# Feed-forward and output projections of a second block: three half-width matmuls per weight tile against one wide and one narrow

## The chip, the cores and the metric

The kernel runs on one core of a Trainium2 chip. The metric is the device time of one execution in microseconds (us); the time before is 1900.26 us, the median of three executions (1900.05 to 1903.23). TensorE is called PE in the profile, its weight loads PEld, VectorE DVE, ScalarE ACT, GpSimd POOL, and SyncE, which starts the transfers, SP.

## What is computed

Two blocks are applied one after the other to 256 tokens of width 1024, in float32. The first block (two layers of retention, neighbourhood attention and grouped attention) is not touched by the change. The second block is what matters here:

```python
def swiglu(x, w_in, w_out):
    g, u = jnp.split(x @ w_in, 2, axis=-1)
    return (jax.nn.silu(g) * u) @ w_out
...
    for i in range(DEPTH):
        h = h + 0.5 * swiglu(rms_norm_2(h, ffn1_norm[i]), ffn1_w_in[i], ffn1_w_out[i])
        hn = rms_norm_2(h, mix_norm[i])
...
            m = recurrent_mixer(hn, ...)
...
            m = spatial_gating_mixer(hn, ...)
        h = h + m
        h = h + 0.5 * swiglu(rms_norm_2(h, ffn2_norm[i]), ffn2_w_in[i], ffn2_w_out[i])
    return rms_norm_2(h, final_norm)
```

`DEPTH` is 2, the hidden width of a feed-forward 2816, that of a mixer 1024. So there are four feed-forwards (each with `w_in` of 1024 x 5632 and `w_out` of 2816 x 1024) and two mixers, each of which ends with a product by an output matrix of 1024 x 1024.

## The kernel before

**Tiling.** Activations lie transposed, 128 features on the partitions and 256 tokens (`T`) in the free dimension: eight tiles for a width of 1024 (`NK`), 22 for the hidden width (`NF`). Every factor of a product is split into two fp32r parts, a rounded hi and the remainder lo (`split`, L387: ACT rounds, DVE subtracts). A product of a weight tile of 128 x 128 and an activation tile takes three matmuls (`mm3`, L400): weight hi by activation hi, weight hi by activation lo, weight lo by activation hi, all added into the same 256 columns of PSUM. Each matmul has its own weight load. `proj` (L439) runs `mm3` over all k tiles of a contraction.

**Stages.** The names in the profile carry the stage: `f` (first feed-forward, input side) and `f0b` (its output side), `mix0r`, `mix0y`, `mix0yb` (recurrent mixer and its output side), `fb` and `fb0b`, `fa` and `fa1b`, `mix` and `mix1b` (spatial mixer), `fb` again and `fb1b`. On the input side (`ffn`, L1251) one step makes one 128-row chunk of the hidden tensor: `project2` (L1207) puts the gate product g and the up product u into the two halves of one PSUM bank of 512 columns, 8 k tiles by three matmuls each, and `ffn_evac` (L1269) multiplies the whole bank by the reciprocal norm `rs`, applies Silu to the g half, multiplies by the u half and splits the result into hi and lo. On the output side (`back`, L1214) each of eight output tiles j has a PSUM bank, half of it used, with 22 k tiles (8 for a mixer); then one DVE instruction adds it to the residual `x[j]`, ACT squares that for the next norm, and `scaled` (L1190) makes the next stage's hi and lo inputs from it: ACT writes hi, DVE lo, side by side in one tile of 512 columns. The weights come in through three `raw` buffers of 1 MB (`wload`), and are split into four `wh` and four `wl` buffers of 1024 columns (`wsplit`, L422). There are eight PSUM banks and 60 tiles in pool `r`.

**Order.** Nothing is issued while the program text runs. A recorder (L96 to L335) keeps every operation, puts them into an order with a list scheduler that knows their dependences, the buffers and a nominal duration for each, and issues each engine's operations in that order; so every instruction has line L335 in the profile, and changed shapes move the order of all engines. At run time each engine takes its own list strictly in order. The scheduler treats operations on one PSUM bank as dependent in program order, so the u half of a bank comes after its g half.

## Time and profile before

| | |
|---|---|
| time, median of 3 executions | 1900.26 us (1900.05 to 1903.23) |
| the profiled execution's own time | 1902.64 us |
| its span, first to last instruction | 1900.9 us |
| PE busy | 1858.4 us, 13632 matmuls |
| DVE busy | 1432.9 us, 2177 instructions |
| ACT busy | 1066.3 us, 1704 instructions |
| mean granted TensorE clock | 0.994 of full speed (2.4 GHz) |
| DMA | 291.95 MB, 154 GB/s |

The profiled execution lies 2.38 us above the median; 1.74 us of its time lie outside its span. Busy time of PE counts overlapping matmuls once; the mean ns of a matmul is its own length from issue to end, longer than the distance from one to the next. How far apart two start is read from the timeline.

### The profile page before, as it was taken

How to read it: one execution, taken by the hardware profiler on the slowest of the kernel's cores; microseconds unless marked ns; L12 is line 12 of the kernel's file. 1: busy time of each engine (PE TensorE's matmuls, PEld its weight loads, DVE VectorE, ACT ScalarE, POOL GpSimd, SP SyncE). 2: the span in 40 equal slices, each digit the busy share in tenths (PEclk: the TensorE clock that was granted, in tenths of full speed). 3: DMA queues.
4: the chain of work that ended last, by engine and by line, in shares of the span. 5: the costliest groups of instructions: out<-in, count | busy, mean ns of one | idle time of the engine just before them, and what ended most of it. 6: DMA issues, size and time to landing. Idle time of an engine off the chain costs nothing.

```text
span 1900.9 us, 33415 instructions
## 1 busy us (share of the span) xinstructions
PE 1858.4 (98%) x13632; PEld 1739.5 (92%) x13632; DVE 1432.9 (75%) x2177; ACT 1066.3 (56%) x1704; POOL 209.7 (11%) x152
## 2 busy tenths in 40 slices
PE   6999999999999999999999999999999999999998
PEld 4888777777789889999999999999999999999998
DVE  7778978799857699999787668876656665777654
ACT  4656555656445597766565447754445444755443
POOL 0123323133300022222000000000000010000000
PEclk9999999999999999999999999999999999999999
DMA  9332443524343324434655566355555555545552
GB/s 321 119 97 93 128 148 101 155 88 123 102 153 100 89 78 116 124 106 146 209 178 188 190 194 200 111 201 187 179 183 180 188 181 193 190 157 176 181 188 98
DMA packets 336249, 291.95 MB, mean 154 GB/s; under 512 B 9184, under 2 KB 325728, under 8 KB 336096
## 3 DMA queue, kind: packets, MB, share of 16 engines
q1 hardware_dynamic: 336096, 289.82, 48.0%
q8 instruction: 107, 1.75, 0.4%
q14 instruction: 46, 0.38, 0.1%
HBM read 288.75 MB, written 1.05 MB: 152 GB/s over the span
## 4 chain that ended last, share of the span: by engine, by line
PE 87%; DVE 8%; ACT 2%; issue 1%; POOL 1%; DMA 0%; SPq 0%; DVEq 0%; POOLq 0%; ACTq 0%
PE fb_ps L335 13%; PE L0m_ps L335 7%; PE f_ps L335 7%; PE fa_ps L335 7%; PE L0n_ps L335 5%; PE L1m_ps L335 5%; PE L1r_ps L335 4%; PE L0r_ps L335 4%; PE fb1b_ps L335 3%; PE L1n_ps L335 3%; PE fa1b_ps L335 3%; PE fb0b_ps L335 3%; PE f0b_ps L335 3%; PE mix_ps L335 3%; PE L0out_ps L335 2%; PE L0in_ps L335 2%
## 5 line engine op out<-in xcount | busy, mean ns | idle before, releaser
L335 PE MATMUL fb_ps<-fb_r,fb_wh 128*128 128x256 f32 x1408 | 253.8, 283 | 0.0
L335 PEld LDWEIGHTS fb_ps<-fb_r,fb_wh 128*128 128x128 f32 x1408 | 219.6, 192 | 0.1
L335 PE MATMUL fb_ps<-fb_r,fb_wl 128*128 128x256 f32 x704 | 198.9, 283 | 0.0
L335 ACT CAST fb_wh<-fb_raw 128x1024 fp32r<-128x1024 f32 x88 | 92.2, 1047 | 123.0 <-PE fb_ps L335 89.3
L335 DVE TENSOR_TENSOR fb_wl<-fb_raw,fb_wh 128x1024 fp32r<-128x1024 f32 x88 | 107.7, 1224 | 65.1 <-ACT fb_wh L335 65.0
L335 PEld LDWEIGHTS fb_ps<-fb_r,fb_wl 128*128 128x128 f32 x704 | 135.0, 192 | 0.0
L335 PE MATMUL f_ps<-f_r,f_wh 128*128 128x256 f32 x704 | 127.2, 283 | 0.0
L335 PE MATMUL fa_ps<-fa_r,fa_wh 128*128 128x256 f32 x704 | 126.9, 283 | 0.0
L335 PE MATMUL L0m_ps<-L0in_r,L0m_wh 128*128 128x512 f32 x384 | 121.5, 395 | 0.0
L335 PEld LDWEIGHTS f_ps<-f_r,f_wh 128*128 128x128 f32 x704 | 109.8, 192 | 0.1
L335 PEld LDWEIGHTS fa_ps<-fa_r,fa_wh 128*128 128x128 f32 x704 | 109.8, 192 | 0.1
L335 PE MATMUL fa_ps<-fa_r,fa_wl 128*128 128x256 f32 x352 | 99.4, 283 | 0.0
L335 PE MATMUL f_ps<-f_r,f_wl 128*128 128x256 f32 x352 | 99.3, 283 | 0.0
L335 PEld LDWEIGHTS L0m_ps<-L0in_r,L0m_wh 128*128 128x128 f32 x384 | 71.9, 189 | 16.7 <-issue 1.6
L335 ACT CAST fa_wh<-fa_raw 128x1024 fp32r<-128x1024 f32 x44 | 46.1, 1047 | 63.5 <-PE fa_ps L335 39.7
L335 DVE TENSOR_TENSOR fa_wl<-fa_raw,fa_wh 128x1024 fp32r<-128x1024 f32 x44 | 53.8, 1224 | 35.4 <-ACT fa_wh L335 35.4
L335 POOL MEMSET mix_r<- 128x128 f32 (+1 forms) x36 | 7.7, 239 | 653.4 <-DVE fa_r L335 490.4
L335 DVE TENSOR_TENSOR L0g_r<-L0g_r,L0g_r 128x512 f32<-128x512 f32 (+3 forms) x116 | 72.4, 670 | 7.6 <-ACT L0g_r L335 5.4
L335 ACT CAST f_wh<-f_raw 128x1024 fp32r<-128x1024 f32 x44 | 46.1, 1048 | 56.4 <-PE f_ps L335 35.6
L335 PE MATMUL L0m_ps<-L0in_r,L0m_wl 128*128 128x512 f32 x192 | 75.0, 391 | 0.0
L335 ACT ACT_TABLE_LOAD x56 | 71.8, 1283 | 3.1 <-PE L0out_ps L335 1.4
L335 DVE TENSOR_TENSOR f_wl<-f_raw,f_wh 128x1024 fp32r<-128x1024 f32 x44 | 53.7, 1221 | 24.9 <-ACT f_wh L335 24.8
(506 smaller groups left out, 5729.7 us busy)
## 6 DMA issues: line engine op xcount, KB each, us to landing
fb_raw<-in_ffn_w_in_dram SPq DMA_DIRECT2D x44, 1024.0 KB, 5.2
f_raw<-in_ffn_w_in_dram SPq DMA_DIRECT2D x22, 1024.0 KB, 5.1
fa_raw<-in_ffn_w_in_dram SPq DMA_DIRECT2D x22, 1024.0 KB, 5.2
ada_raw<-in_ada_w_dram SPq DMA_DIRECT2D x32, 512.0 KB, 4.5
L0m_raw<-in_w_in_dram SPq DMA_DIRECT2D x24, 512.0 KB, 3.9
L1m_raw<-in_w_in_dram SPq DMA_DIRECT2D x24, 512.0 KB, 4.3
L0in_raw<-in_ada_w_dram SPq DMA_DIRECT2D x32, 256.0 KB, 6.0
f0b_raw<-in_ffn_w_out_dram SPq DMA_DIRECT2D x8, 1024.0 KB, 5.3
```

The source lines that it names most:

```text
L335: getattr(getattr(self.real, eng), method)(*a, **k)
```

## The change

On the feed-forwards' input side, and on the output side of feed-forwards and mixers, one matmul of 512 columns takes weight hi by the activation tile [hi|lo] in place of two of 256. All 8 (or 6) k tiles of a weight buffer are taken so, and only then come the matmuls of weight lo by activation hi, 256 columns each, into the first half of the bank. The second half holds weight hi by activation lo, and is added later: on the input side ACT copies it to SBUF and DVE adds the first half (`halves`, twice per chunk, as g and u now have a bank each), and the multiplication by `rs` then reads SBUF; on the output side DVE updates `x[j]` twice, once per half. The hidden tiles are kept as one [hi|lo] tile per 128 rows. The input sides of the mixers and the first block keep three matmuls of 256 columns (`project_pair` is the old `project2`).

```diff
+    def proj_wide(self, out, w, x, k0=0, start=True, stop=True):
+
+        n = len(w)
+        for k in range(n):
+            self.mm(out, lhsT=w[k][0], rhs=x[k0 + k], start=start and k == 0, stop=False)
+        for k in range(n):
+            self.mm(out[:, :T], lhsT=w[k][1], rhs=x[k0 + k][:, :T], start=False, stop=stop and k == n - 1)
+
+    def halves(self, out, ps):
+
+        c = self.f()
+        self.nc.scalar.copy(c[:, :T], ps[:, T:])
+        self.tt(out, ps[:, :T], c[:, :T], ALU.add)
...
+    def project2(self, cols, a):
+
+        out = []
+        for wr in cols:
+            ps = self.ps()
+            self.proj_wide(ps, self.wsplit(wr), a)
+            out.append(ps)
+        return out
+
+    def sums2(self, out, pss, rs):
+
+        for i, ps in enumerate(pss):
+            self.halves(out[:, T * i : T * i + T], ps)
+        self.tt(self.v2(out), self.v2(out), self.b2(rs), ALU.mult)
...
-                self.proj(po[j0 + i][:, :T], self.wsplit(raw[:, :, P * i : P * i + P]), hid, k0,
-                          start=k0 == 0, stop=k0 + kn == kt)
+                self.proj_wide(po[j0 + i], self.wsplit(raw[:, :, P * i : P * i + P]), hid, k0,
+                               start=k0 == 0, stop=k0 + kn == kt)
...
-                self.stt(x[j], po[j][:, :T], scale, x[j], ALU.mult, ALU.add)
+                for h in (slice(0, T), slice(T, T2)):
+                    self.stt(x[j], po[j][:, h], scale, x[j], ALU.mult, ALU.add)
...
-                ps = self.project2(w_in, [g[:, :, c], u[:, :, c]], a)
+                ps = self.project2([g[:, :, c], u[:, :, c]], a)
...
+    def ffn_evac(self, pss, rs, hid):
+        t = self.f()
+        self.sums2(t, pss, rs)
+        s = self.f()
+        self.act(s[:, :T], t[:, :T], AF.Silu)
+        self.tt(s[:, :T], s[:, :T], t[:, T:], ALU.mult)
+        hid.append(self.split_wide(s[:, :T]))
...
-            hid.append(self.pair(s, T))
+            hid.append(self.split_wide(s[:, :T]))
```

How the order moves is shown at three places; a name's last number is its buffer.

PE, in the middle of the third feed-forward's input side (`fa`); before, three matmuls for each activation tile `fa_r`:

```order
L335 MATMUL fa_ps_2896<-fa_r_2832,fa_wh_2897 128x256 x2
L335 MATMUL fa_ps_2896<-fa_r_2832,fa_wl_2898 128x256
L335 MATMUL fa_ps_2896<-fa_r_2833,fa_wh_2897 128x256 x2
L335 MATMUL fa_ps_2896<-fa_r_2833,fa_wl_2898 128x256
L335 MATMUL fa_ps_2896<-fa_r_2834,fa_wh_2897 128x256 x2
L335 MATMUL fa_ps_2896<-fa_r_2834,fa_wl_2898 128x256
```

The same place in the changed kernel, at the end of the eight wide matmuls of one bank:

```order
L335 MATMUL fa_ps_3044<-fa_r_2965,fa_wh_3045 128x512
L335 MATMUL fa_ps_3044<-fa_r_2966,fa_wh_3045 128x512
L335 MATMUL fa_ps_3044<-fa_r_2959,fa_wl_3046 128x256
L335 MATMUL fa_ps_3044<-fa_r_2960,fa_wl_3046 128x256
L335 MATMUL fa_ps_3044<-fa_r_2961,fa_wl_3046 128x256
L335 MATMUL fa_ps_3044<-fa_r_2962,fa_wl_3046 128x256
```

A bank is now one product, g or u; the weight lo is first read eight wide matmuls after the weight hi.

DVE, one chunk of the same stage before (`fa_wl` are weight remainders, the row that reads `fa_ps` is the multiplication by `rs`, the two of 128x256 are the gating product and the hidden tile's remainder):

```order
L335 TENSOR_TENSOR fa_r_2901<-fa_ps_2896,fa_r_2851 128x512
L335 TENSOR_TENSOR fa_wl_2918<-fa_raw_2911,fa_wh_2917 128x1024
L335 TENSOR_TENSOR fa_r_2902<-fa_r_2902,fa_r_2901 128x256
L335 TENSOR_TENSOR fa_wl_2923<-fa_raw_2910,fa_wh_2922 128x1024
L335 TENSOR_TENSOR fa_r_2895<-fa_r_2902,fa_r_2894 128x256
L335 TENSOR_TENSOR fa_r_2908<-fa_ps_2903,fa_r_2851 128x512
```

and one chunk in the changed kernel, where the rows that read `fa_ps` are the two additions and the row of 128x512 after them the multiplication:

```order
L335 TENSOR_TENSOR fa_r_3074<-fa_ps_3068,fa_r_3075 128x256
L335 TENSOR_TENSOR fa_wl_3097<-fa_raw_3091,fa_wh_3096 128x1024
L335 TENSOR_TENSOR fa_r_3065<-fa_r_3064,fa_r_3065 128x256
L335 TENSOR_TENSOR fa_r_3074<-fa_ps_3071,fa_r_3076 128x256
L335 TENSOR_TENSOR fa_r_3074<-fa_r_3074,fa_r_2983 128x512
L335 TENSOR_TENSOR fa_wl_3105<-fa_raw_3090,fa_wh_3104 128x1024
L335 TENSOR_TENSOR fa_r_3077<-fa_r_3077,fa_r_3074 128x256
L335 TENSOR_TENSOR fa_r_3085<-fa_ps_3079,fa_r_3086 128x256
```

The chunk has two rows more, and each addition stands between two weight remainders in the queue.

PE where the spatial mixer's output side starts (`mix1b`); the hidden tiles k = 0, 1, 2 are `mix_r_3228`, `mix_r_3230`, `mix_r_3233` before:

```order
L335 MATMUL mix1b_ps_3247<-mix_r_3228,mix1b_wh_3248 128x256 x2
L335 MATMUL mix1b_ps_3247<-mix_r_3228,mix1b_wl_3249 128x256
L335 MATMUL mix1b_ps_3250<-mix_r_3228,mix1b_wh_3251 128x256 x2
L335 MATMUL mix1b_ps_3247<-mix_r_3230,mix1b_wh_3248 128x256
L335 MATMUL mix1b_ps_3250<-mix_r_3228,mix1b_wl_3252 128x256
L335 MATMUL mix1b_ps_3250<-mix_r_3230,mix1b_wh_3251 128x256
L335 MATMUL mix1b_ps_3256<-mix_r_3228,mix1b_wh_3257 128x256 x2
L335 MATMUL mix1b_ps_3256<-mix_r_3228,mix1b_wl_3258 128x256
L335 MATMUL mix1b_ps_3256<-mix_r_3230,mix1b_wh_3257 128x256
```

In the changed kernel k = 0 to 7 are `mix_r_3426`, `_3428`, `_3431`, `_3433`, `_3436`, `_3438`, `_3441`, `_3443`:

```order
L335 MATMUL mix1b_ps_3445<-mix_r_3426,mix1b_wh_3446 128x512
L335 MATMUL mix1b_ps_3448<-mix_r_3426,mix1b_wh_3449 128x512
L335 MATMUL mix1b_ps_3454<-mix_r_3426,mix1b_wh_3455 128x512
L335 MATMUL mix1b_ps_3457<-mix_r_3426,mix1b_wh_3458 128x512
L335 MATMUL mix1b_ps_3445<-mix_r_3428,mix1b_wh_3446 128x512
L335 MATMUL mix1b_ps_3445<-mix_r_3431,mix1b_wh_3446 128x512
L335 MATMUL mix1b_ps_3445<-mix_r_3433,mix1b_wh_3446 128x512
L335 MATMUL mix1b_ps_3448<-mix_r_3428,mix1b_wh_3449 128x512
L335 MATMUL mix1b_ps_3445<-mix_r_3436,mix1b_wh_3446 128x512
L335 MATMUL mix1b_ps_3445<-mix_r_3438,mix1b_wh_3446 128x512
```

Before, three matmuls of each bank are there for a hidden tile, and one of them needs only its hi part; now one, which reads hi and lo together. DVE at that place in the changed kernel (the first row reads the last PSUM result of the mixer, the rows that write 3428 to 3443 are the remainders):

```order
L335 SCALAR_TENSOR_TENSOR mix_r_3442<-mix_ps_3439,vecs,mix_r_3319 128x256
L335 TENSOR_TENSOR mix_r_3432<-mix_r_3432,mix_r_3409 128x256
L335 TENSOR_TENSOR mix_r_3437<-mix_r_3437,mix_r_3416 128x256
L335 TENSOR_TENSOR mix_r_3440<-mix_r_3440,mix_r_3423 128x256
L335 TENSOR_TENSOR mix_r_3442<-mix_r_3442,mix_r_3423 128x256
L335 TENSOR_TENSOR mix_r_3428<-mix_r_3427,mix_r_3428 128x256
L335 TENSOR_TENSOR mix_r_3433<-mix_r_3432,mix_r_3433 128x256
L335 TENSOR_TENSOR mix_r_3436<-mix_r_3435,mix_r_3436 128x256
L335 TENSOR_TENSOR mix_r_3438<-mix_r_3437,mix_r_3438 128x256
L335 TENSOR_TENSOR mix_r_3441<-mix_r_3440,mix_r_3441 128x256
L335 TENSOR_TENSOR mix_r_3443<-mix_r_3442,mix_r_3443 128x256
```

The remainder of k = 1 is the sixth row, four products behind the row that reads PSUM, and the others follow it.

## Rows read from the trace of the kernel before

**Rows 1.** The page, part 1: an engine's busy us, share of the span, instructions.
```profile
PE 1858.4 (98%) x13632; PEld 1739.5 (92%) x13632; DVE 1432.9 (75%) x2177; ACT 1066.3 (56%) x1704; POOL 209.7 (11%) x152
```

**Rows 2.** Busy time by stage: stretch, its length, busy us (instructions) of PE, PEld, DVE, ACT, POOL, granted clock.
```profile
1164.30:1243.70 79.40, 76.59 (x628) 75.57 (x628) 69.67 (x130) 65.76 (x124) 0.00 (x0) 1.00 0.46 150
...
1434.20:1561.30 127.10, 127.10 (x1060) 127.05 (x1059) 86.66 (x114) 63.51 (x94) 5.59 (x32) 1.00 0.57 187
```

**Rows 3.** The chain that ended last, second block: start us, us, what, matmuls.
```profile
973.38 127.56 PE f_ps L335 x1060
...
1100.93 63.36 PE f0b_ps L335 x528
...
1434.17 127.14 PE fa_ps L335 x1058
...
1561.31 63.36 PE fa1b_ps L335 x528
```

**Rows 4.** Timeline of PE, second block's feed-forward: start us, us, instruction, count.
```profile
1499.94 0.40 PE L335 MATMUL fa_ps<-fa_r,fa_wh 128*128 128x256 f32 x2
...
1507.14 0.40 PE L335 MATMUL fa_ps<-fa_r,fa_wh 128*128 128x256 f32 x2
```

**Rows 5.** Timeline of PE, first block's merge, 512 columns per matmul.
```profile
519.74 0.61 PE L335 MATMUL L0m_ps<-L0in_r,L0m_wh 128*128 128x512 f32 x2
...
526.54 0.62 PE L335 MATMUL L0m_ps<-L0in_r,L0m_wh 128*128 128x512 f32 x2
```

**Rows 6.** Timeline of PE, first block, both widths in turn.
```profile
626.01 0.40 PE L335 MATMUL L1r_ps<-L0out_r,L1r_wh 128*128 128x512 f32 x1
626.25 0.40 PE L335 MATMUL L1r_ps<-L1r_wh,L0out_r 128*128 128x256 f32 x2
626.49 0.28 PE L335 MATMUL L1r_ps<-L1r_wl,L0out_r 128*128 128x256 f32 x1
626.61 0.40 PE L335 MATMUL L1r_ps<-L0out_r,L1r_wh 128*128 128x512 f32 x1
```

**Rows 7.** Groups by form, third feed-forward: busy us, mean ns, idle before and releasers.
```profile
L335 DVE TENSOR_TENSOR fa_wl<-fa_raw,fa_wh 128x1024 fp32r<-128x1024 f32 x42 | 51.4, 1224 | 31.7 <-ACT fa_wh L335 31.7
...
L335 ACT CAST fa_wh<-fa_raw 128x1024 fp32r<-128x1024 f32 x41 | 42.9, 1047 | 57.5 <-PE fa_ps L335 39.7 <-issue 13.5 <-DMA fa_raw<-in_ffn_w_in_dram 4.2
...
L335 DVE TENSOR_TENSOR fa_r<-fa_ps,fa_r 128x512 f32<-128x512 f32 x21 | 14.4, 690 | 5.3 <-PE fa_ps L335 5.3
...
L335 DVE TENSOR_TENSOR fa_r<-fa_r,fa_r 128x256 f32<-128x256 f32 x21 | 8.7, 418 | 0.0
...
L335 ACT CAST fa_r<-fa_r 128x256 fp32r<-128x256 f32 x21 | 8.3, 401 | 0.0
```

**Rows 8.** PE's waits in the second block: us in total, times, longest.
```profile
PE mix0yb_ps L335 <- DVE mix0y_r L335: 1.0, 1, 1.0
PE mix0yb_ps L335 <- DVE mix0yb_r L335: 0.9, 1, 0.9
PE mix0yb_ps L335 <- DVE mix0yb_wl L335: 0.5, 1, 0.5
PE mix0yb_ps L335 <- ACT mix0yb_wh L335: 0.4, 1, 0.4
PE fb1b_ps L335 <- DVE fb1b_r L335: 0.3, 1, 0.3
```

**Rows 9.** Timeline of PE (first row) and DVE where mix1b starts.
```profile
1677.21 0.40 PE L335 MATMUL mix1b_ps<-mix_r,mix1b_wh 128*128 128x256 f32 x2
...
1677.47 0.48 DVE L335 SCALAR_TENSOR_TENSOR mix_r<-mix_ps,vecs,mix_r 128x256 f32<-128x256 f32 x1
...
1677.87 3.43 DVE L335 TENSOR_TENSOR mix_r<-mix_r,mix_r 128x256 f32<-128x256 f32 x10
...
1682.35 0.42 DVE L335 SCALAR_TENSOR_TENSOR L0out_m<-mix1b_ps,L0out_m 128x256 f32<-128x256 f32 x1
```

More of the change, by code (lines that the diff above doesn't have):

```diff
@@ L1197, in scaled, with split_wide @@
             self.stt(lo, x[j], wj, hi.bitcast(F32), ALU.mult, ALU.subtract)
-            out.append((hi, lo))
+            out.append(t)
         return out
+    def split_wide(self, src):
+        t = self.r()
+        self.split(t[:, :T], t[:, T:], src)
+        return t
     def b2(self, r):
@@ L1205, in v2, with project_pair @@
         return t.rearrange("p (a b) -> p a b", a=2)
-    def project2(self, w, cols, a):
+    def project_pair(self, cols, a):
         ps = self.ps()
+        x = [(t[:, :T], t[:, T:]) for t in a]
         for i, wr in enumerate(cols):
-            self.proj(ps[:, T * i : T * i + T], self.wsplit(wr), a)
+            self.proj(ps[:, T * i : T * i + T], self.wsplit(wr), x)
         return ps
+    def project2(self, cols, a):
[9 more added lines that the diff above has]
+        self.tt(self.v2(out), self.v2(out), self.b2(rs), ALU.mult)
     def back(self, w_out, hid, x, scale, halves=0, then=None):
@@ L1255, in ffn @@
             (u,) = self.wload([self.wk(w_in, D_FF + P * f, 256)])
-            th, tl = self.r(), self.r()
             for i in range(2):
                 c = slice(P * i, P * i + P)
-                ps = self.project2(w_in, [g[:, :, c], u[:, :, c]], a)
+                ps = self.project2([g[:, :, c], u[:, :, c]], a)
                 if f == 0 and i == 1:
                     rs = mk_rs()
-                    self.ffn_evac(first, rs, th, tl, 0, hid)
+                    self.ffn_evac(first, rs, hid)
                 elif f == 0:
@@ L1265, in ffn @@
                     continue
-                self.ffn_evac(ps, rs, th, tl, i, hid)
+                self.ffn_evac(ps, rs, hid)
         return self.back(w_out, hid, x, 0.5, then=then)
-    def ffn_evac(self, ps, rs, th, tl, i, hid):
-                t = self.f()
-                self.tt(self.v2(t), self.v2(ps), self.b2(rs), ALU.mult)
-                s = self.f()
-                self.act(s[:, :T], t[:, :T], AF.Silu)
-                self.tt(s[:, :T], s[:, :T], t[:, T:], ALU.mult)
-                c = slice(T * i, T * i + T)
-                self.split(th[:, c], tl[:, c], s[:, :T])
-                hid.append((th[:, c], tl[:, c]))
+    def ffn_evac(self, pss, rs, hid):
[5 more added lines that the diff above has]
+        hid.append(self.split_wide(s[:, :T]))
     def softplus(self):
@@ L1330, in chain @@
             (raw,) = self.wload([self.wk(w, D + P * jp, 256)])
-            ps = self.project2(w, [raw[:, :, P * i : P * i + P] for i in range(2)], a)
+            ps = self.project_pair([raw[:, :, P * i : P * i + P] for i in range(2)], a)
             if jp == 0:
@@ L1375, in gated @@
             (raw,) = self.wload([self.wk(w, P * jp, 256)])
-            ps = self.project2(w, [raw[:, :, P * i : P * i + P] for i in range(2)], a)
+            ps = self.project_pair([raw[:, :, P * i : P * i + P] for i in range(2)], a)
             y = self.f()
@@ L1381, in gated @@
             self.tt(y, y, hs[jp // 2], ALU.mult)
-            hi, lo = self.pair(y, 512)
             for i in range(2):
-                hid[jp + i] = (hi[:, T * i : T * i + T], lo[:, T * i : T * i + T])
+                hid[jp + i] = self.split_wide(y[:, T * i : T * i + T])
         self.early = EARLY
@@ L1419, in spatial @@
                     tk = slice(P * t, P * t + P)
-                    self.mm3(ps[:, T * t : T * t + T], (a[k][0][:, tk], a[k][1][:, tk]), ws[k], k == 0, k == NK - 1)
+                    self.mm3(ps[:, T * t : T * t + T], (a[k][:, :T][:, tk], a[k][:, T:][:, tk]), ws[k], k == 0, k == NK - 1)
             if cc == 0:
@@ L1433, in spatial @@
             (raw,) = self.wload([self.wk(w, P * jp, 256)])
-            ps = self.project2(w, [raw[:, :, P * i : P * i + P] for i in range(2)], a)
+            ps = self.project_pair([raw[:, :, P * i : P * i + P] for i in range(2)], a)
             u = self.f()
```

## Prediction

> **What bounds the kernel now.** The page's first part comes first: PE is busy for 98% of the span, DVE for 75% [rows 1]. Busy is not yet the bound, so the chain that ended last is read next, from the start of the second block at 973 us. It shows one engine with nothing between: 127.56 us of PE for the first feed-forward's input side, 63.36 us for its output side, and the same in the later ones, stage after stage [rows 3]. 63.36 us for 528 matmuls are 120.0 ns each; 127.14 us for 1056 and the norm's two matmuls are the same pace. The table by stage agrees: in the third feed-forward PE is busy 127.10 of 127.10 us at granted clock 1.00 (2.4 GHz), while DVE works 86.66 us and ACT 63.51 us [rows 2]. The list of PE's waits in the whole second block has five entries between 0.3 and 1.0 us, 3.1 us together, four of them in the recurrent mixer's output side and one at the end [rows 8]. So in the 915 us where the change acts, the time is the number of matmuls times their distance, as long as DVE and ACT keep ahead.
>
> Then the distance itself, from the timeline. In the second block the listed rows from 1499.94 to 1507.14 us hold 20 rows of two matmuls and 20 of one, 60 of 256 columns in 7.20 us: 120.0 ns each [rows 4]. In the first block's merge, matmuls of 512 columns with the same kind of weight load run from 519.74 to 526.54, 30 in 6.80 us: 226.7 ns each [rows 5]. Twice the columns cost 106.7 ns more, not 120.0. So a matmul pays 106.7 ns per 256 columns and 13.3 ns besides, whatever its width. Where both widths take turns nothing is added: a wide one starts at 626.01, two narrow ones at 626.25, one at 626.49, the next wide one at 626.61 [rows 6], that is 0.24, 0.24 and 0.12 us.
>
> **What the change gives.** A pair of weight tile and activation tile costs 3 x 120.0 = 360.0 ns now, and 226.7 + 120.0 = 346.7 ns after: 13.3 ns less, with the same columns streamed and one weight load fewer. The pairs: a feed-forward has 44 products of 8 k tiles on the input side and 8 of 22 on the output side, 528; four have 2112; two mixers' output sides add 2 x 64. **2240 pairs x 13.3 ns = 29.9 us.** All of it lies on PE, which is the chain there. Bounds for the price of a wide matmul in these stages: 226.7 ns [rows 5] and twice 120.0 [rows 4], at which the gain is nothing. I take 226.7, since rows 5 have the same shape and types, fp32r weights, 512 contiguous columns and one whole bank, and rows 6 mix the widths.
>
> The Trainium skill, "TensorE: Matmul & The Clock Gate", section "Wait — 56ns, not 53.3ns?", puts the fixed cost of a warm matmul at about 2.5 ns beyond its columns. By it the change would save 2240 x 2.5 = 5.6 us; the measured distances of both widths [rows 4, 5] disagree with it, and the measurement decides.
>
> **What it adds beside PE.** A chunk of the input side gets two ACT copies of 256 from PSUM and two DVE additions of 256. No row shows just these: a 256-wide DVE product is 0.42 us in SBUF, a 512-wide one out of PSUM 0.69 [rows 7], a 256-wide update out of PSUM 0.42 [rows 9]; a 256-wide ACT rounding is 0.40 [rows 7]. I take 0.42 and 0.40; the upper ends are 0.69 for DVE and, for ACT, half of its 1.05 us for 1024 columns. A stage has 44 of each: DVE 86.7 + 44 x 0.42 = 105.2 us, ACT 63.5 + 17.6 = 81.1, both within the 122.0 us that PE then needs (352 x 346.7 ns). With 0.69 DVE has 117, still below. The multiplication by rs keeps its 512 columns. Two banks per chunk instead of one still leave four chunks in the eight banks, and a bank is now emptied before rs is needed, so the first chunks don't wait for the norm. Cost on the path: nothing, and the cover is PE's 5.55 us per chunk. The weights' low parts are needed 8 x 0.227 = 1.8 us later than their high parts, which helps. Transfers keep their order and sizes; they come 2% faster at a DMA share of 0.57 [rows 2].
>
> **What goes onto the path.** Three places.
>
> First, the spatial mixer's output side. Now PE starts it at 1677.21, the last result leaves PSUM on DVE from 1677.47, and then come ten rows of 0.34 us, products and remainders, until 1681.3 [rows 9]; PE doesn't wait, because it takes many matmuls that need only the hi part of a hidden tile. A wide matmul needs both. The changed order gives PE four wide matmuls (0.9 us, to 1678.1), then k = 1, whose remainder is the fifth of the ten rows: 1677.87 + 5 x 0.34 = 1679.6. **1.5 us lost**; afterwards remainders come every 0.34 us and PE asks for one in 0.23 to 0.45, so nothing more. Bounds: 0, if DVE is earlier, and 3.2, if PE waits until 1681.3.
>
> Second, the recurrent mixer's output side, where PE already idles 2.8 us of 79.4 [rows 2, 8] on DVE's tiles and on weight splits. What PE saves there (64 x 13.3 ns = 0.85 us) is mostly waited for again: **0.65 us lost**, between 0 and 0.85.
>
> Third, the end. After the last matmul DVE has two updates for each of the last two output tiles instead of one: 2 x 0.42 [rows 9], both in front of the last transposes: **0.8 us lost**, 0.4 if one is hidden.
>
> At the other stage starts the last two inputs come up to 0.8 us later, by the extra updates, with a weight remainder of 1.2 us queued between. After its last matmul DVE needs three updates, that remainder and the input's own: 3 x 0.42 + 1.22 + 0.48 = 3.0 us. The new orders put 19 or 20 wide matmuls, 4.3 us, ahead of the first that reads them. Cost: nothing; 1.9 us per start if the cover is gone.
>
> **The sum.** 29.9 - 1.5 - 0.65 - 0.8 = 26.9 us. Against the profiled execution 1902.64 - 26.9 = 1875.7 us; that execution stands 2.4 us above the median, so for the median 1900.26 - 26.9 = **1873.4 us**, 1.4% faster.
>
> **Rivals.**
>
> *Late starts.* At five stage starts (four feed-forwards, the spatial mixer) PE waits for the last two inputs. For it: DVE's queue is in order, and two updates and a weight remainder stand in front of them. Against: the cover of 4.3 us. Price: 5 x 1.9 = 9.5 us, so 1882.9.
>
> *DVE takes over, and the kernel gets slower.* In a stage DVE's 86.7 us of work already come with 37 us in which it stood, 31.7 for ACT's roundings and 5.3 for PE [rows 7], 124 of 127. An addition is late when its copy is late, and the weight remainder queued behind it is late with it. If the waits stay as they are, a stage takes 86.7 + 37.0 + 18.5 = 142.2 us instead of 127.1; four stages lose 60 us, output sides and mixers still give 11.1 back, the three places take 2.95: about 1952. It decides from 21.9 us of waits per stage on (127.1 - 105.2), and above 16.8 it eats into the gain. Against it: ACT's roundings stand 39.7 us for PE to free weight buffers [rows 7], so DVE's waits are mostly those of engines that run ahead, and shrink when there is more to do.
>
> *Only a small fixed cost goes.* If the 13.3 ns belong to something that the wide form keeps here, and 2.5 ns per pair go, 5.6 us less 2.95 us leave 1897.6. Against: rows 4 and 5.
>
> *It doesn't do what it says.* The wide form streams at the pace of two narrow ones: 1900.26 + 2.95 = 1903.2. Against: rows 5.
>
> **How the numbers follow.** About 0.2%, 3.8 us, is what a measurement of this kernel can tell from no change. My forecast (1868 to 1879) gets 0.74, late starts and partial delays of the evacuation (1879 to 1893) 0.15, the small fixed cost 0.03, no effect 0.03, the slower case 0.05. Faster by over 0.2% (below 1896.5) is the first two and part of the third, 0.90; within 0.2% 0.05; slower 0.05. The range starts where nothing is lost and the recurrent mixer's 2.8 us of idle time go too, 1900.26 - 29.9 - 2.8 = 1867.6; it ends past the late starts (1882.9) with the bounds of the first place (1.7 more): 1885. What is left out is 0.11 for the last three rivals and a few hundredths of partial delays.
>
> **What the profile after would show.** PE with 13632 - 2240 = 11392 matmuls. In the timeline of a feed-forward, wide rows 0.227 us apart and then narrow ones 0.120 apart; chain pieces of about 122.4 us for an input side and 61.0 for an output side, still PE alone. DVE near 105 us and ACT near 81 in a stage. PE's waits: one of about 1.5 us at the start of mix1b, those of mix0yb a little longer, none of note in a feed-forward. It is wrong if wide matmuls stand 0.24 us apart, if the chain of a feed-forward holds DVE or ACT pieces, or if waits for fa_r or fa_wl appear in every chunk.

## The result, and the profile after

| | before | after |
|---|---|---|
| median, us | 1901.72 | 1882.11 |
| lowest to highest, us | 1900.05 to 1903.23 | 1880.28 to 1883.12 |
| profiled execution, us | 1902.64 | 1883.12 |
| its span, us | 1900.9 | 1881.1 |

Both columns are four executions, taken side by side. The ratio is 0.9896 with an interval of 0.9879 to 0.9913: about 1.0% faster, 19.6 us between the medians. The sum of the prediction had 26.9 us, so some 7 us of the expected gain have to be found.

The first part of the page of the changed kernel shows the matmuls that went (13632 before, [rows 1]) and the work that came to DVE and ACT:

```profile
PE 1837.5 (98%) x11392; PEld 1623.5 (86%) x11392; DVE 1504.0 (80%) x2405; ACT 1114.0 (59%) x1884; POOL 209.9 (11%) x152
```

The chain that ended last, from the start of the second block on (start us, us, engine and tile, matmuls), answers to [rows 3]:

```profile
975.44 123.76 PE f_ps L335 x708
1099.20 61.52 PE f0b_ps L335 x352
...
1239.23 123.28 PE fb_ps L335 x706
1362.52 61.50 PE fb0b_ps L335 x352
1424.01 123.37 PE fa_ps L335 x706
1547.38 61.48 PE fa1b_ps L335 x352
1608.86 52.23 PE mix_ps L335 x434
1661.12 2.90 DVE mix_r L335 x8
1664.06 21.72 PE mix1b_ps L335 x124
1685.78 123.32 PE fb_ps L335 x706
1809.10 62.98 PE fb1b_ps L335 x364
```

The feed-forwards are PE alone, as forecast. But their pieces are 123.3 to 123.8 us where 122.4 were expected, and 61.5 where 61.0 were. The block starts at 975.44 instead of 973.38, though nothing ahead of it was changed.

Two stretches by stage, with the columns of [rows 2] (length, busy us of PE, PEld, DVE, ACT, POOL, granted clock): the recurrent mixer and the third feed-forward's input side.

```profile
1160.70:1239.20 78.50, 76.71 (x564) 73.27 (x563) 71.07 (x140) 66.89 (x128) 0.00 (x0) 0.98 0.46 148
1424.00:1547.40 123.40, 123.40 (x708) 108.56 (x707) 101.37 (x159) 74.97 (x136) 5.21 (x32) 1.00 0.59 193
```

DVE has 101.4 us of work in 123.4 and ACT 75.0; PE is never without work. In the mixer the granted clock is 0.98 where it was 1.00, and PE is as long busy with 564 matmuls as it was with 628.

PE's waits in the second block, beside [rows 8]:

```profile
PE mix0yb_ps L335 <- DVE mix0y_r L335: 1.7, 1, 1.7
PE mix1b_ps L335 <- DVE mix_r L335: 1.6, 1, 1.6
PE fb1b_ps L335 <- DVE fb1b_r L335: 1.1, 2, 0.8
```

PE's timeline inside the third feed-forward, beside [rows 4] (start us, us, instruction, count):

```profile
1480.18 2.00 PE L335 MATMUL fa_ps<-fa_r,fa_wh 128*128 128x512 f32 x8
1482.02 1.11 PE L335 MATMUL fa_ps<-fa_r,fa_wl 128*128 128x256 f32 x8
1482.97 2.00 PE L335 MATMUL fa_ps<-fa_r,fa_wh 128*128 128x512 f32 x8
1484.81 1.12 PE L335 MATMUL fa_ps<-fa_r,fa_wl 128*128 128x256 f32 x8
1485.77 2.00 PE L335 MATMUL fa_ps<-fa_r,fa_wh 128*128 128x512 f32 x8
```

From one bank's first wide matmul to the next one's are 2.79 us, 349 ns a pair. Eight times 226.7 and eight times 120.0 would be 2.774. The starts of the single matmuls in the same trace, averaged over the full banks of this stage, show where the 20 ns are: the distances behind the eight wide ones are 233.3, 235.5, 228.4, 232.6, 230.8, 226.8, 226.8 and 226.7 ns, those behind the narrow ones 113.5, 119.2 and then 120.0. (For the first one 233.3 is the value of the output sides; in this stage one bank with a wait of 0.2 us lifts its mean.) The first five wide matmuls are slow, by 27 ns together, and the first narrow one gives 6.5 back. On an output side, where no bank is emptied in the meantime, the distances are the same within 0.3 ns; in its parts of six wide and six narrow ones the loss is 20 ns too.

**Where the 26.9 us went.** In the second block, from its start in the chain to the end of the span, 927.5 us became 905.7: 21.8 us gained. The other 2.1 us are the later start. So in the block 5.1 us are missing: 288 runs of wide matmuls (176 banks of the input sides, 96 parts of the feed-forwards' output sides, 16 of the mixers') with 20 ns each make 5.7 us, and the three places where something was to be added cost about what the sum had, somewhat less in the first mixer.

The later start came in code that both kernels have. Against the trace of before, the same matmuls of the first block slip by 0.8 us near 27 us of the span and by 0.95 us between 420 and 422, and hardly elsewhere. The second place is visible by stage: first before, then after.

```profile
420.00:440.00 20.00, 18.79 (x109) 13.28 (x110) 17.95 (x26) 9.63 (x15) 1.90 (x1) 0.91 0.67 198
```

```profile
420.00:440.00 20.00, 17.59 (x101) 11.84 (x101) 17.01 (x24) 8.96 (x14) 0.00 (x0) 0.83 0.63 185
```

In that execution the granted clock stood longer at half there, and near 27 us it rose later. In all the profiled executions of this study the second block's piece of the chain began between 971.4 and 975.5 us, with the same first block. That is the spread of the runs, not the change. For this reason the table below gives the second block by itself.

### The profile page after: what moved, and what is told of

Same layout as the page of the kernel before. It is cut to its first block, busy times and chain, and to the rows that moved or that the text cites. A ratio compares the mean times of both kernels' runs of the same rounds, so it can differ in the third digit from the quotient of the medians.

```text
span 1881.1 us, 29398 instructions
## 1 busy us (share of the span) xinstructions
PE 1837.5 (98%) x11392; PEld 1623.5 (86%) x11392; DVE 1504.0 (80%) x2405; ACT 1114.0 (59%) x1884; POOL 209.9 (11%) x152
## 4 chain that ended last, share of the span: by engine, by line
PE 88%; DVE 7%; ACT 2%; issue 1%; DMA 1%; POOL 1%; SPq 0%; DVEq 0%; POOLq 0%; ACTq 0%
PE fb_ps L335 13%; PE L0m_ps L335 8%; PE f_ps L335 7%; PE fa_ps L335 7%; PE L0n_ps L335 5%; PE L1m_ps L335 5%; PE L1r_ps L335 4%; PE L0r_ps L335 4%; PE fb1b_ps L335 3%; PE L1n_ps L335 3%; PE f0b_ps L335 3%; PE fb0b_ps L335 3%; PE fa1b_ps L335 3%; PE mix_ps L335 3%; PE L0out_ps L335 2%; PE L0g_ps L335 2%
## 5 line engine op out<-in xcount | busy, mean ns | idle before, releaser
L335 PE MATMUL fb_ps<-fb_r,fb_wh 128*128 128x512 f32 x704 | 176.6, 393 | 0.0
L335 PEld LDWEIGHTS fb_ps<-fb_r,fb_wh 128*128 128x128 f32 x704 | 126.7, 189 | 22.8
L335 PE MATMUL fb_ps<-fb_r,fb_wl 128*128 128x256 f32 x704 | 98.1, 282 | 0.0
L335 PE MATMUL f_ps<-f_r,f_wh 128*128 128x512 f32 x352 | 88.7, 393 | 0.0
L335 PE MATMUL fa_ps<-fa_r,fa_wh 128*128 128x512 f32 x352 | 88.4, 393 | 0.0
L335 ACT CAST fa_wh<-fa_raw 128x1024 fp32r<-128x1024 f32 x44 | 46.1, 1050 | 47.6 <-PE fa_ps L335 29.9
L335 PEld LDWEIGHTS fa_ps<-fa_r,fa_wh 128*128 128x128 f32 x352 | 63.4, 189 | 11.4
L335 DVE TENSOR_TENSOR fa_wl<-fa_raw,fa_wh 128x1024 fp32r<-128x1024 f32 x44 | 53.8, 1223 | 24.4 <-ACT fa_wh L335 18.1
L335 PEld LDWEIGHTS f_ps<-f_r,f_wh 128*128 128x128 f32 x352 | 63.4, 189 | 11.4
L335 PE MATMUL L1m_ps<-L0out_r,L1m_wh 128*128 128x256 f32 x384 | 71.8, 283 | 0.0
L335 ACT CAST L0m_wh<-L0m_raw 128x1024 fp32r<-128x1024 f32 (+1 forms) x48 | 39.9, 837 | 53.1 <-PE L0m_ps L335 35.0
L335 DVE TENSOR_TENSOR L0n_r<-L0n_r,L0n_r 128x512 f32<-128x512 f32 (+2 forms) x104 | 69.8, 714 | 1.1 <-POOL L0n_r L335 0.5
```

The source lines that it names most:

```text
L335: getattr(getattr(self.real, eng), method)(*a, **k)
```

## The experiments

Theory: TensorE's distances set the time, the wide form saves 13.3 ns a pair, and a fixed 20 ns is lost at each change from a run of narrow matmuls to wide ones. Rivals: the loss belongs to the start of a bank, to each wide matmul, or to the evacuation that reads the banks meanwhile; or the gain is not one of the width at all.

All runs in one table. "Second block" goes from its first matmul to the last instruction of the profiled execution; "fa" and "fa1b" are the input and the output side of the third feed-forward, from first matmul to first matmul.

| kernel | median us | ratio to before (95%) | second block us | fa | fa1b |
|---|---|---|---|---|---|
| before | 1901.72 | | 927.60 | 127.14 | 63.36 |
| after | 1882.11 | 0.9896 (0.9879 to 0.9913) | 905.77 | 123.37 | 61.48 |
| alternate | 1876.77 | 0.9859 (0.9845 to 0.9874) | 900.89 | 122.68 | 61.04 |
| two_banks | 1880.64 | 0.9882 (0.9867 to 0.9896) | 906.29 | 122.92 | 61.26 |
| no_halves | 1879.69 | 0.9880 (0.9865 to 0.9894) | 905.67 | 123.36 | 61.48 |
| input_only | 1884.16 | 0.9902 (0.9885 to 0.9918) | 910.08 | 123.39 | 63.36 |
| three_narrow | 1902.27 | 1.0001 (0.9992 to 1.0011) | 927.28 | 127.26 | 63.36 |
| fours | 1884.17 | 0.9910 (0.9895 to 0.9925) | 908.51 | 123.87 | 61.65 |
| twos | 1879.40 | 0.9886 (0.9869 to 0.9902) | 905.94 | 123.06 | 61.35 |
| alternate_mix0 | 1876.77 | 0.9870 (0.9851 to 0.9890) | 906.39 | 122.47 | 61.05 |
| all_wide | 1882.13 | 0.9889 (0.9874 to 0.9905) | 911.34 | 122.68 | 61.05 |
| after_again | 1880.77 | 0.9886 (0.9871 to 0.9900) | 905.78 | 123.37 | 61.48 |
| alternate_again | 1877.29 | 0.9868 (0.9852 to 0.9884) | 903.96 | 122.68 | 61.05 |
| mixers_narrow | 1879.22 | 0.9880 (0.9865 to 0.9895) | 904.18 | 123.37 | 61.48 |

### Is the gain one of the width? three_narrow

```diff
 (proj_wide)
-        for k in range(n):
-            self.mm(out, lhsT=w[k][0], rhs=x[k0 + k], start=start and k == 0, stop=False)
-        for k in range(n):
-            self.mm(out[:, :T], lhsT=w[k][1], rhs=x[k0 + k][:, :T], start=False, stop=stop and k == n - 1)
+        for a, b in ((0, 0), (0, 1), (1, 0)):
+            for k in range(n):
+                self.mm(out[:, :T], lhsT=w[k][a], rhs=x[k0 + k][:, T * b : T * b + T],
+                        start=start and a + b + k == 0, stop=stop and a == 1 and k == n - 1)
 (sums2)
-            self.halves(out[:, T * i : T * i + T], ps)
-        self.tt(self.v2(out), self.v2(out), self.b2(rs), ALU.mult)
+            self.tt(out[:, T * i : T * i + T], ps[:, :T], rs[:, :T], ALU.mult)
 (back)
-                for h in (slice(0, T), slice(T, T2)):
+                for h in (slice(0, T),):
```

> The order of the changed kernel (all k of one product, then the next) with matmuls of 256 columns throughout: eight hi x hi, eight hi x lo, eight lo x hi, all into the first half of the bank, so that nothing has to be added later. If the gain is the fixed 13.3 ns of the matmuls that went: 360.0 ns a pair and 2.880 us a bank as before the change, input sides of the feed-forwards 127.1 us, output sides 63.4; in all within 0.2% of the kernel before (1900 to 1905). Rival, the gain (or a part) comes of the order or of weights that change less often: below 1895, at the limit 1882.

1902.27 us, 1.0001 of before. The stages are those of before: 127.26 and 63.36 us. The changed order, with its own banks for gate and up, is worth nothing by itself. The whole gain hangs on the 512 columns.

### Where do the 20 ns belong? alternate and two_banks

In alternate, each k's narrow matmul stands behind its wide one:

```diff
         for k in range(n):
             self.mm(out, lhsT=w[k][0], rhs=x[k0 + k], start=start and k == 0, stop=False)
-        for k in range(n):
             self.mm(out[:, :T], lhsT=w[k][1], rhs=x[k0 + k][:, :T], start=False, stop=stop and k == n - 1)
```

> The wide and the narrow matmul of each k stand one behind the other instead of eight wide, then eight narrow. In the changed kernel a bank of eight pairs takes 2.793 us where its single durations (8 x 226.7 + 8 x 120.0 ns) make 2.774: 20 ns more in each of 280 banks, 5.5 us. Theory A, a fixed loss at every change from narrow to wide: eight changes a bank instead of one, 7 x 20 ns x 280 = +38 us on 1882.1, about 1920, a pair at some 366 ns. Theory A', the loss settles over the five wide matmuls that follow a change and the first of them bears only 6.6 ns, which the narrow one behind it gives back: a pair at 346.7 ns, 1876.6. Rivals B (a loss at the start of each accumulating bank) and C (every wide matmul is 2.5 ns dearer than in the first block's rows): still 349 ns a pair, about 1882.

1876.77 us, 0.9859: theory A' named 1876.6, the fixed loss per change (1920) is out, and so are B and C (1882). That the number is hit so closely is in part luck: this order has a second, slower pace, which came up in later runs (see the versions further on). PE's timeline of alternate in the third feed-forward:

```profile
1479.71 0.39 PE L335 MATMUL fa_ps<-fa_r,fa_wh 128*128 128x512 f32 x1
1479.94 0.28 PE L335 MATMUL fa_ps<-fa_r,fa_wl 128*128 128x256 f32 x1
1480.06 0.39 PE L335 MATMUL fa_ps<-fa_r,fa_wh 128*128 128x512 f32 x1
1480.29 0.28 PE L335 MATMUL fa_ps<-fa_r,fa_wl 128*128 128x256 f32 x1
...
1483.18 0.39 PE L335 MATMUL fa_ps<-fa_r,fa_wh 128*128 128x512 f32 x1
```

From 1479.71 to 1483.18 are ten pairs: 347 ns each, the 346.7 of the prediction. 900.89 us for the second block are 26.7 less than before.

In two_banks the wide matmuls of two banks come first, then the narrow ones of both:

```diff
+        n = len(ws[0])
+        for out, w in zip(outs, ws):
+            for k in range(n):
+                self.mm(out, lhsT=w[k][0], rhs=x[k0 + k], start=start and k == 0, stop=False)
+        for out, w in zip(outs, ws):
+            for k in range(n):
+                self.mm(out[:, :T], lhsT=w[k][1], rhs=x[k0 + k][:, :T], start=False, stop=stop and k == n - 1)
```

> The wide matmuls of two banks (gate and up, or two output tiles) come first, then the narrow ones of both: half as many changes from narrow to wide, as many bank starts. Theory A (loss at a change of width, 20 ns): 140 changes fewer, -2.7 us, about 1879.4; the wide matmuls of the second bank 226.7 ns apart from the first on, two banks in 5.567 us. Rival B (loss at the start of a bank): the second bank's first five wide matmuls are as slow as the first's (233, 236, 228, 233, 231 ns), two banks in 5.587 us, 1882.1. Rival C (each wide matmul): the loss is spread over all sixteen, 1882.1.

Its timeline in the third feed-forward:

```profile
1483.48 3.82 PE L335 MATMUL fa_ps<-fa_r,fa_wh 128*128 128x512 f32 x16
1487.13 2.08 PE L335 MATMUL fa_ps<-fa_r,fa_wl 128*128 128x256 f32 x16
1489.05 3.14 PE L335 MATMUL fa_ps<-fa_r,fa_wh 128*128 128x512 f32 x13
```

Two banks take 5.57 us, theory A's figure. In the single starts the second bank's eight wide matmuls, which begin a bank of their own, are 226.7 ns apart from the first on; only those behind the narrow run are slow. So the loss is not at the start of a bank and not in each wide matmul. The stages gain by it (122.92 against 123.37 us), but the whole came to 1880.64 instead of 1879.4, with an interval that holds both: in the profiled execution PE also waited 1.8 us for f_r and 0.9 for mix_r at two stage starts where the changed kernel doesn't.

### Is it the evacuation? no_halves

```diff
         for i, ps in enumerate(pss):
-            self.halves(out[:, T * i : T * i + T], ps)
-        self.tt(self.v2(out), self.v2(out), self.b2(rs), ALU.mult)
+            self.tt(out[:, T * i : T * i + T], ps[:, :T], rs[:, :T], ALU.mult)
```

> On the input sides of the four feed-forwards the second half of each bank (weight hi x inputs' lo) is left out of the sum: no ACT copy and no DVE add, and the rs multiply reads the bank's first half. The matmuls stay. If the matmuls alone set the pace there: the same time within 0.2% (1880 to 1884), 2.793 us a bank, DVE some 18 us less busy in each input stage. Rival D, the evacuation's reads of the banks are what slows the first five wide matmuls: 2.774 us a bank, 3.4 us faster over 176 banks, about 1878.7. Rival E, DVE's added work delays PE: faster by more than that.

The same stretch by stage, in no_halves:

```profile
1423.20:1546.50 123.30, 123.30 (x708) 108.45 (x707) 87.90 (x139) 65.81 (x95) 5.56 (x32) 1.00 0.59 192
```

DVE has 13.5 us less to do and ACT 9.2, and the stage takes the same time: 123.36 us against 123.37. The median, 1879.69, is just below the expected bracket; the second block, 905.67 against 905.77 us, is the same, and the rest is the first block's spread. The adding of the halves costs nothing on the path. DVE still reads the first half of each bank here, so this run alone doesn't exclude the reads; but the loss is the same on the output sides, where no bank is emptied in the meantime, and so the reads of the banks are not what slows the wide matmuls.

### How long a run does it take? twos and fours

```diff
+        for k1 in range(0, n, 4):
+            ks = range(k1, min(k1 + 4, n))
-        for k in range(n):
+            for k in ks:
                 self.mm(out, lhsT=w[k][0], rhs=x[k0 + k], start=start and k == 0, stop=False)
-        for k in range(n):
+            for k in ks:
                 self.mm(out[:, :T], lhsT=w[k][1], rhs=x[k0 + k][:, :T], start=False, stop=stop and k == n - 1)
```

(in twos a 2 stands for the 4)

> Four wide, four narrow, four wide, four narrow. Alternating single matmuls took 346.7 ns a pair and lost nothing; runs of six, eight and sixteen narrow ones lose 20 ns at the change to wide. If a run of four already brings the whole loss: two changes a bank, up to 20 ns each, a bank 2.807 to 2.813 us, 1886 to 1888. If the loss grows with the run and is half for four: 2.793, 1882. If it needs more than four in a row: 2.774, 1876.6.

> Two wide, two narrow, four times a bank. If any run of narrow ones longer than one brings the loss, cut off after the two wide that follow (6.6 + 9.0 - 6.5 ns a change): 2.810 us a bank, 1887. If the loss grows with the run, a quarter of 20 ns for two: 2.793, 1882. If runs this short lose nothing: 2.774, 1876.6.

Timeline of fours:

```profile
1479.79 1.09 PE L335 MATMUL fa_ps<-fa_r,fa_wh 128*128 128x512 f32 x4
1480.72 0.63 PE L335 MATMUL fa_ps<-fa_r,fa_wl 128*128 128x256 f32 x4
1481.19 1.09 PE L335 MATMUL fa_ps<-fa_r,fa_wh 128*128 128x512 f32 x4
1482.12 0.64 PE L335 MATMUL fa_ps<-fa_r,fa_wl 128*128 128x256 f32 x4
1482.60 1.09 PE L335 MATMUL fa_ps<-fa_r,fa_wh 128*128 128x512 f32 x4
```

and of twos:

```profile
1479.75 0.63 PE L335 MATMUL fa_ps<-fa_r,fa_wh 128*128 128x512 f32 x2
1480.22 0.40 PE L335 MATMUL fa_ps<-fa_r,fa_wl 128*128 128x256 f32 x2
1480.45 0.63 PE L335 MATMUL fa_ps<-fa_r,fa_wh 128*128 128x512 f32 x2
...
1481.84 0.63 PE L335 MATMUL fa_ps<-fa_r,fa_wh 128*128 128x512 f32 x2
```

Fours take 2.81 us a bank, the first of their three cases in pace; the time, 1884.17 us, stayed below its 1886 to 1888. Twos take 0.697 us for two pairs, 2.787 a bank, a little under their middle case, and 1879.40 us. From the single starts the loss at one change is 3.3 ns in runs of two, 14 to 16 in runs of four, and 20 in runs of six, eight and sixteen; per pair that is 1.7, 3.5 to 4, 3.3, 2.5 and 1.3 ns.

These runs shorten the wide stretch together with the narrow one, and the first block of the kernel before, which has no such link, separates the two. There four narrow matmuls between long wide stretches (from 491.96 us) are followed by distances of 233, 236, 229, 232 and 231 ns: four already bring the whole loss. In fours only four wide ones follow, and the first four slow distances less what the narrow ones give back make 15.7 ns. So from four on theory A', cut off where the wide stretch ends, is right; for two it would give some 9 ns where 3.3 were measured, and that stays open.

### The parts: input_only and mixers_narrow

```diff
 (back, input_only)
-                self.proj_wide(po[j0 + i], self.wsplit(raw[:, :, P * i : P * i + P]), hid, k0,
+                self.proj(po[j0 + i][:, :T], self.wsplit(raw[:, :, P * i : P * i + P]), [(t[:, :T], t[:, T:]) for t in hid], k0,
...
-                for h in (slice(0, T), slice(T, T2)):
-                    self.stt(x[j], po[j][:, h], scale, x[j], ALU.mult, ALU.add)
+                self.stt(x[j], po[j][:, :T], scale, x[j], ALU.mult, ALU.add)
```

In mixers_narrow the same stands under `if kt == NK`, which is true in the mixers alone.

> The output sides go back to three narrow matmuls a pair and one update a tile; only the input sides are wide. 832 pairs lose 360.0 - 349.2 = 10.8 ns each, +9.0 us; what came back are the waits at the starts of the output sides, 1.6 us in mix1b, some 0.7 of mix0yb's 1.7, 0.8 of fb1b: -3.1. About +5.9 on 1882.1, 1888.0. If the late starts are not worth that much (the work behind them was waiting anyway): 1891. If the output sides' gain was already lost elsewhere: 1883 or less.

> The changed kernel with the output sides of both mixers back at three narrow matmuls a pair and one update a tile; the feed-forwards stay wide. 128 pairs x 10.8 ns = 1.4 us lost. If the late starts are the price of the wide form there, mix1b goes from 24.2 to 23.25 us and the first mixer from 78.5 to 76.7, as in the run with only the input sides wide: 2.8 us faster than the changed kernel, about 1879.3. If not, 1883.5.

input_only came to 1884.16 us, not 1888. Its output sides are back at 63.36 us, as expected, and mix1b at 23.25 (24.22 in the changed kernel). The recurrent mixer is the miss: 76.72 us, 1.8 shorter than in the changed kernel, where the expectation had let its waits and its pairs cancel. The second block is 4.3 us longer than the changed kernel's, against 5.9 expected, and in the profiled execution it began 2.7 us earlier.

mixers_narrow: 1879.22 us beside 1880.77 of the changed kernel on the same chip, 1.6 us faster (second block 904.18 against 905.78) where 2.8 were expected. The first mixer went to 77.80 us instead of 76.7, mix1b to 23.25. PE's waits there:

```profile
PE mix0yb_ps L335 <- ACT mix0y_r L335: 0.7, 1, 0.7
PE mix0yb_ps L335 <- DVE mix0yb_r L335: 0.4, 1, 0.4
PE mix0yb_ps L335 <- DVE mix0y_r L335: 0.2, 1, 0.2
```

So with all wide matmuls of a bank in a row, the two mixers' output sides together lose more by their starts than their 128 pairs give, 1.6 us of the second block; the executions of the two kernels overlap (1878.97 to 1880.61 and 1879.66 to 1881.13 us).

But it is not the width that makes mix1b late. three_narrow also runs one bank through all its k before the rest, with matmuls of 256 columns alone, and its mix1b takes 24.19 us, as in the changed kernel:

```profile
PE mix1b_ps L335 <- ACT mix_r L335: 0.9, 1, 0.9
```

And alternate, which is wide but takes the narrow matmul of each k before the next k, has mix1b at 23.18 us, a little under the narrow 23.25, with a wait of 0.6 us. So the late start comes with the order, which needs the later hidden tiles early. In the first mixer the price of the wide form can't be told apart: with narrow matmuls on its output side it took 79.4 us (before), 77.9 (alternate_mix0), 77.8 (mixers_narrow), 77.2 (three_narrow) and 76.7 (input_only), with wide ones 78.2 to 79.3, and the order of DVE and ACT is another in each.

### Versions further on: alternate_mix0, all_wide, and three kernels on one chip

alternate_mix0 has the order of alternate and the narrow form in the recurrent mixer's output side. all_wide has in addition:

```diff
-            ps = self.project_pair([raw[:, :, P * i : P * i + P] for i in range(2)], a)
+            ps = self.project2([raw[:, :, P * i : P * i + P] for i in range(2)], a)
...
-            self.tt(self.v2(rt), self.v2(ps), self.b2(S["rs"]), ALU.mult)
+            self.sums2(rt, ps, S["rs"])
```

> Wide and narrow alternate as in the run of that name (1876.77 us, 0.9859 of before), and the output side of the first mixer goes back to three narrow matmuls a pair and one update a tile. With the output sides narrow the first mixer took 76.7 us, with the alternating order 78.4: 1.7 us faster than alternating alone, about 1875, 0.985 of before. If the waits at the start of mix0yb come from elsewhere: 64 pairs x 13.3 ns = 0.85 us slower than alternating, 1877.6.

> As alternate_mix0, and the input sides of both mixers are wide too, alternating, with the ACT copy and the DVE add for their 24 banks. 24 x 8 = 192 pairs x 13.3 ns = 2.6 us where TensorE sets the pace: about 1872.5, 0.9835 of before. If DVE and ACT, which the first mixer's chain of small steps loads most, take the added work onto the path: 24 x (0.37 + 0.42) us is 19 us of added work, of which the first mixer has two thirds, and the time is anywhere from 1875 to 1885, slower than alternate_mix0.

all_wide: 1882.13 us, the second case. PE's longest waits in its first mixer:

```profile
PE mix0y_ps L335 <- DVE mix0y_r L335: 2.5, 1, 2.5
...
PE mix0yb_ps L335 <- DVE mix0yb_r L335: 1.6, 1, 1.6
```

From its first matmul to the next stage's it takes 84.8 us, against 77.9 in alternate_mix0, which differs by the mixers' input sides alone. There too the chain goes over ACT and DVE for much of the stage. So where DVE and ACT bound a stage, the added work (16 copies of 0.37 us and 16 additions of 0.42) made it 6.9 us longer, and the matmuls saved did not make up for it.

alternate_mix0: 1876.77 us, no faster than alternating alone, with executions from 1873.20 to 1883.54. In the profiled one (1883.54) the recurrent mixer is 0.5 us shorter, where 1.7 were expected, but f takes 125.68 us, f0b 62.03, fb 124.84 and fb0b 62.08, where the run of alternate has 123.67, 61.07, 122.54 and 61.08. The matmuls and their order in these stages are the same. The single starts show why: from one wide matmul to the next are 353.3 ns in the first four feed-forward stages (the expectation below says three), and 346.7 in the later ones. The next three kernels were run for that.

> The alternating order once more. A profiled run of it took 346.7 ns a pair in all stages, one of alternate_mix0 353.8 ns in the first three feed-forward stages and 346.7 behind them. If each stage falls into one of two paces when TensorE starts it, the runs lie between 1873 (all at 346.7) and 1884 (most at 353.8; 2112 pairs x 7.1 ns = 15 us between the ends), with a median of 1875 to 1880, under the changed kernel's, and wider than its. If the slower pace belongs to alternate_mix0 alone: 1873 to 1878.5 again.

> The changed kernel as it is, beside the next two on one chip: 1880 to 1884 us, 0.9885 to 0.991 of before; 349.2 ns a pair in every feed-forward stage, as the loss comes at the same place of each bank.

alternate_again: 1877.29 us, 1876.31 to 1879.02, all below the changed kernel's 1879.66 to 1881.13 on the same chip. Both paces are in its trace. The input side of the first feed-forward, ten pairs between two lines:

```profile
1039.82 0.28 PE L335 MATMUL f_ps<-f_r,f_wl 128*128 128x256 f32 x1
...
1043.36 0.28 PE L335 MATMUL f_ps<-f_r,f_wl 128*128 128x256 f32 x1
```

and that of the third:

```profile
1479.79 0.28 PE L335 MATMUL fa_ps<-fa_r,fa_wl 128*128 128x256 f32 x1
...
1483.26 0.28 PE L335 MATMUL fa_ps<-fa_r,fa_wl 128*128 128x256 f32 x1
```

3.54 us and 3.47 us for the same ten pairs at granted clock 1.00. The pace belongs to the alternating order and not to alternate_mix0. In the single starts the slow one repeats every three pairs, 361, 350 and 349 ns: it loses 20 ns in three pairs, as much as one change from a long narrow run, and is then slower than the changed kernel's 349.2. The pace changes, with hardly an exception, only where something breaks the alternation: at the start of an input stage, and again 12 to 18 us into it, where the norm's two matmuls come in between. From there it holds for more than 440 pairs, far into the output side behind it. In alternate's own run, too, the third feed-forward was slow for its first 12 us, until the norm's matmuls. Which of the two comes up stays open. after_again repeats the changed kernel within 0.02 us in every stage of the second block, so its own loss is fixed.

Alternating is the fastest of the versions by its medians (0.9859 and 0.9868 of before), with a wider spread. On one chip its interval (0.9852 to 0.9884) overlaps that of the changed kernel (0.9871 to 0.9900), while the executions of the two don't.

## Why the prediction was right, and where it was mis-sized

- **What bounds it.** PE's matmul distances, from the start of the block to its end. It held: PE's busy time fills every feed-forward stage before and after, no_halves takes 13.5 us of DVE work out of a stage without moving it, and three_narrow shows that the gain comes with the width, not with the new order or the banks.
- **2240 pairs x 13.3 ns = 29.9 us.** This is the step that was mis-sized. Measured were 10.8 ns on the input sides (15.25 us for 1408 pairs) and 10.6 on the output sides (5.58 us for 528), some 24 us in all. The price of the wide matmul, 226.7 ns, was taken from [rows 5], where all are wide, and its place beside narrow ones from [rows 6], where only one or two narrow ones lie between. Both hold: the sixth to eighth wide matmul of a bank stand 226.7 ns apart, and the alternating order gave 346.7 ns a pair at the faster of its paces. What no listed row of before showed was a run of eight narrow ones followed by wide ones, and there the first five are slow. The order of the matmuls, which the prediction took to be of no account, cost 5.7 us by the count of runs; the alternating order got 4.9 of them back.

  The loss could have been read before the change. [rows 6] have the wide matmul 0.24 us before the next, where 0.227 was assumed; the prediction read this as nothing added. And the first block of the kernel before has long narrow runs followed by wide ones (start us, us, instruction, count):

```profile
797.79 1.60 PE L335 MATMUL L1g_ps<-L1g_r,L1gk_r 128*128 128x256 f32 x12
799.23 0.63 PE L335 MATMUL L1n_ps<-L0out_r,L1n_wh 128*128 128x512 f32 x2
...
800.39 0.39 PE L335 MATMUL L1n_ps<-L0out_r,L1n_wl 128*128 128x512 f32 x1
...
801.75 0.39 PE L335 MATMUL L1n_ps<-L0out_r,L1n_wl 128*128 128x512 f32 x1
```

  The twelve narrow ones stand 120 ns apart. From 799.23 to 800.39 are five wide matmuls, 232 ns each; from 800.39 to 801.75 six, 226.7 each. These are the five slow distances of the changed kernel, in code that the change doesn't touch.
- **The small fixed cost.** 1897.6 us is out: a pair lost 10.8 ns, not 2.5, and 13.3 where nothing else was in the way. The Trainium skill's about 2.5 ns per warm matmul ("TensorE: Matmul & The Clock Gate", section "Wait — 56ns, not 53.3ns?") doesn't fit these fp32r matmuls; the measurement decides.
- **mix1b, 1.5 us.** The list of waits has 1.6 us, and the place is the one described: four wide matmuls, then the wait for DVE's remainders, which come as ten rows in 3.43 us as before [rows 9].

```profile
1661.40 1.09 PE L335 MATMUL mix1b_ps<-mix_r,mix1b_wh 128*128 128x512 f32 x4
1664.06 2.34 PE L335 MATMUL mix1b_ps<-mix_r,mix1b_wh 128*128 128x512 f32 x9 [1.57 <-DVE mix_r L335]
```

- **The recurrent mixer, 0.65 us lost of 0.85.** The stage went from 79.4 to 78.5 us, so about 0.7 us better than that. But not by the step that was named, and so by luck: PE's busy time did not fall (76.59 to 76.71 us for 64 fewer matmuls), since behind the wait of 1.7 us the granted clock was for a while at half. The waits themselves became fewer. In no_halves, with the same output side and a wait of 1.8 us at the same place, the clock stayed at 1.00 and PE was busy for 75.7 us, but it waited 0.7 us more elsewhere, and the stage took 78.3.
- **The end, 0.8 us.** From the first matmul of fb1b to the end 73.22 us became 72.11: 1.1 us, where 176 pairs at 10.8 ns give 1.9. That is 0.8 lost, and the place is the one described: PE's waits for DVE behind the last weight matmul went from 0.3 us [rows 8] to 1.1.
- **Evacuation at no cost.** DVE was to have 105 us of work in an input stage and ACT 81; they have 101 and 75. DVE's waits for ACT's roundings fell from 31.7 us [rows 7] to 18.1 when there was more to do, so DVE did not take over (the group of the weights' remainders in the third feed-forward: busy us, mean ns, idle before and releasers). In all_wide's first mixer, where DVE's and ACT's work is part of the chain, added work did lengthen the stage.

```profile
L335 DVE TENSOR_TENSOR fa_wl<-fa_raw,fa_wh 128x1024 fp32r<-128x1024 f32 x42 | 51.3, 1223 | 20.7 <-ACT fa_wh L335 18.1 <-PE fb0b_ps L335 2.5
```

- **Late starts at the feed-forwards.** None of note; the cover of wide matmuls was enough.

Put together, the 905.7 us of the block are explained within half a microsecond. The remaining distance between 1873.4 and 1882.1 us is the higher median of before in the comparison (1901.72 instead of 1900.26) and the first block's spread of some 2 us in the profiled execution. That the range, 1867.6 to 1885.0, holds the measured time is luck: its upper part was there for late starts and partial delays of the evacuation (1879 to 1893, chance 0.15). The time lies in that part, outside the forecast of 1868 to 1879 that had 0.74, and 0.8 us from the 1882.9 of the late starts, which did not happen in the feed-forwards.

## What to carry to other kernels

Where TensorE's matmul distances set the time, joining two matmuls that share a weight tile saves the fixed part of a matmul, here 13.3 ns of 120 at best and 10.8 in the order used, and work added to engines with room cost nothing here. Price the new sequence from rows in which the widths follow each other in the order that the kernel will use: single prices, or a row with one change, miss what a run of one width does to the next. Where a stage waits for its inputs, look at which of them the new order needs first: running one bank through all its k asks for the last inputs early, at either width. And where other engines bound a stage, don't give them more work to save matmuls.

## What was not expected of the hardware

- After a run of 256-column matmuls the next five of 512 columns start up to 9 ns later each than the 226.7 ns at which they otherwise follow. Four narrow ones are enough, and a wide stretch shorter than five cuts the loss off (20 ns per change in equal runs from six on, 14 to 16 in runs of four; in runs of two it is 3.3, less than such a cut explains). It does not depend on a new bank or on its evacuation. Why was not found.
- Strict alternation of the two widths has two stable paces, 346.7 ns a pair without a loss and 353.3 with 20 ns lost every three pairs, in the same program at granted clock 1.00; which of them holds is settled anew where the alternation is broken.
- The first block, with the same instructions, ended up to 4.0 us apart in different profiled executions; in the pair compared, 1.8 of its 2.1 us came at two places where the granted clock rose later or stood longer at half.
